# Moving low parts, layer norm sums and norm products from GpSimd to VectorE in a hybrid attention layer

## The chip, the cores and the metric

The kernel runs on one core of a Trainium2 chip. The metric is the device time of one execution, in microseconds (us). A run's time is what is compared; the profile below is of one execution, whose span (first to last instruction) is a little shorter than its time. TensorE's clock has two levels here, 1.2 and 2.4 GHz; the granted clock in the rows is the share of the higher one.

## What is computed

One decoder layer on x of 1024 tokens by 1024 channels in float32. From xn = RMSNorm(x) one projection w_in gives the inputs of three branches:

```
A: sparse attention: 8 query heads in 2 groups, RMS-normed q and k;
   compressed keys/values from blocks of 32 tokens (stride 16) through a small MLP,
   selected blocks (all 16 are taken at this length), and a window of 512; three gates
B: u = a * sigmoid(ag); causal depthwise convolution over 31 taps;
   LayerNorm over 512 channels; silu; projection
C: cross attention of 4 heads into 256 memory tokens, RMS-normed q and k
merged = gate_A * A + gate_B * B + gate_C * C;  h = x + merged @ w_out
out = h + (silu(hn @ w_gate) * (hn @ w_up)) @ w_down,  hn = RMSNorm(h)
```

## The kernel before

**Products in three parts.** A float32 operand is split into a high part (a cast to fp32r, on ScalarE, called ACT in the profile) and a low part (the operand minus the high part). `split` (L130) does both; the low part runs on VectorE unless an engine is given. `mm3` (L151) makes high x high, high x low and low x high, three matmuls for each product. A weight unit (`unit`, L246) is a DMA of 512 KB into a staging tile of two buffers (`st`, for the fill `fst` of one), a cast of 128x1024 and a low part of 128x1024. `col_unit` and `row_units` call it; `row_units` makes two units.

**Order of the work.** The kernel is written as one long list of steps. A planner (the Tile layer) lays the instructions of each engine out in one fixed order before the run, by a priority that follows the order of the text and by its own simulation of times. On the chip every engine works through its list in that order, and waits by semaphores. SyncE (SP) issues all DMAs, in its order too.

1. *Start.* The row norm_mix is loaded (L317 to L319), spread over the partitions by a matmul with ones and scaled by ACT into `gmix` (L324, L325). Four tiles of 256 tokens of x are loaded (L320, L327), normed (`norm_pair`, L200: square and sum on ACT, L205; scaling on VectorE, L207), transposed on TensorE (L216) and split. Along with it goes the projection of the first half of the memory queries.
2. *Convolution inputs* (L368): per channel tile two weight units, four projections, sigmoid, product on VectorE (L378).
3. *The taps.* 31 taps for each of four channel tiles (L361), 124 multiply-adds of some 128x1000 on VectorE (L364, L365), accumulate the convolution. They have a low priority (TAP) and are spread by hand over the following projections (L572 to L579): tap j is laid out after the matmul at which the share of columns passed reaches j / (124 + TAP_LEAD), TAP_LEAD = 24. The columns counted go from the end of the first channel tile to the last query projection.
4. *Compression* (L404 to L460): two weight units with low parts on GpSimd (POOL), additions of the positions (L417, L420, on GpSimd), the MLP.
5. *Memory* (L463 to L563): the memory tokens are normed and projected to keys and values by eight units, then two rounds of memory attention, beside which the remaining query projections run. The low parts of their units, the products of a norm with its gain (`gain_mul`, L292) and the scaling of the softmax (L521) are on GpSimd.
6. *Layer norm of the convolution* (L581 to L609): a sum over four channel tiles (`sum4`, L581, on GpSimd), the mean by a matmul with ones, subtraction (L593), squares, a second sum on GpSimd, the variance, products with the reciprocal root on GpSimd (L606), silu, and a DMA of the result.
7. *Keys and values* of the selected and window branches (L612 to L636), four units with low parts on GpSimd, eight gain products.
8. *Attention* (L639 to L768), with scalings on GpSimd (L653, L661).
9. *The fill* (L778 to L791): 24 units of the merge gate projection, each 48 matmuls of 512 columns (two halves of the tokens, 8 blocks of channels, 3 parts), with the lowest priority of all (FILL). The first N_EARLY = 12 go wherever TensorE has a gap; the others are spread over the attention by hand. Each unit's low part is on GpSimd. There are two buffers for fill units (`fsl`) and one PSUM bank (`pf`), copied out by ACT (L790).
10. Merge, output projection and the feed-forward part follow; nothing in them is changed.

```
def split(hi, lo, src, eng=None):
    nc.scalar.copy(hi, src)
    sub(eng or nc.vector, lo, src, hi.bitcast(F32))
...
        along = products[first_tap:]
        total, run, j = sum(n for _, n in along), 0, 0
        for m, n in along:
            while j < len(taps) and run * (len(taps) + TAP_LEAD) >= j * total:
```

Of the kernel before, what the change touches and what calls it, by code (L numbers as in the profile page):

```python
# [11 lines left out]
AF = mybir.ActivationFunctionType  # L12
OP = mybir.AluOpType
# [4 lines left out]
P = 128  # L18
S = 1024
D = 1024  # L20
# [8 lines left out]
C_Q, C_KC, C_VC, C_KV, C_G, C_A, C_AG, C_QM, C_GM = 0, 512, 640, 768, 1280, 1304, 1816, 2328, 2840  # L29
# [2 lines left out]
ORDER = mybir.DependencyInfo(mybir.DependencyClass.NoSync, mybir.DependencyReason.DATA)  # L32
N_EARLY = 12
WB, LAG, SPREAD = 6, 4, 97
TAP_LEAD = 24
N_MAIN, N_W, N_F = 16, 3, 2


# [1 line left out]
def hybrid_layer_kernel(  # L40
# [4 lines left out]
    nc = tc.nc  # L45
    x, mem, out = x[0], mem[0], out[0]
    w_in, w_mem_kv, w_out = w_in[0], w_mem_kv[0], w_out[0]
# [41 lines left out]
    def t2(shape, dt=F32, p=P):  # L89
        return t2p.tile([p] + shape, dt, tag="t2", name=nm("t2"))  # L90
# [135 lines left out]
    def rows2(src, r0):  # L226
        xs = slab([2, D], F32)
        for tt in range(2):
            nc.sync.dma_start(xs[:, tt, :], src[r0 + tt * P:r0 + (tt + 1) * P, :])
        return xs  # L230
# [25 lines left out]
    def col_unit(w, c0, n=P, alloc=wslab, eng=None, load=False):  # L256
        return unit(w[:, c0:c0 + n].rearrange("(k p) c -> p k c", p=P), [w.shape[0] // P, n], alloc, eng,
                    load)

    def row_units(w, c0, alloc=wslab, eng=None):  # L260
        return [unit(w[u * 512:(u + 1) * 512, c0:c0 + 256].rearrange("(k p) c -> p k c", p=P), [4, 256], alloc, eng)
                for u in range(2)]
# [7 lines left out]
    def tok_proj(ws, tp, act=xn, alloc=bank):  # L270
        o = alloc([2, 256])
        for tt in range(2):
            t = 2 * tp + tt
            half, a = t // 4, (t % 4) * P
            for k in range(KT):
                w = ws[k // 4]
                mm3(o[:, tt, :], act(0, k, half, a, a + P), act(1, k, half, a, a + P), w[:, 0, k % 4, :],
                    w[:, 1, k % 4, :], k == 0, k == KT - 1)
        return o
# [11 lines left out]

    def gain_mul(t, g):  # L292
        a, h, d = t.shape[1:]
        nc.gpsimd.tensor_tensor(t, t, g[:, None, None, :].to_broadcast([P, a, h, d]), op=OP.mult)


    def head_norms(raw, gain):
# [15 lines left out]
    def raw_proj(ws, tp, dest):  # L313
        ps = tok_proj(ws, tp).rearrange("p t (h d) -> p t h d", h=dest.shape[2])
        nc.scalar.copy(dest[:, 2 * tp:2 * tp + 2], ps)

    g1 = [t2([512], p=1) for _ in range(2)]  # L317
    for half in range(2):
        nc.sync.dma_start(g1[half], norm_mix[:, half * 512:(half + 1) * 512])  # L319
    xin = [rows2(x, 0)]  # L320
    gmix = t4([D])
    for half in range(2):
        b = bank([512])
        nc.tensor.matmul(b, ones[0:1, :], g1[half], start=True, stop=True)  # L324
        nc.scalar.activation(gmix[:, half * 512:(half + 1) * 512], b, AF.Copy, scale=512.0)  # L325
    ws = row_units(w_in, C_QM)
    xin += [rows2(x, tp * 256) for tp in range(1, 4)]  # L327
    nc.sync.dma_start(gm, mem_qk_norm.to_broadcast([P, 2, P]))
# [1 line left out]
    QMQ = {}  # L330
# [71 lines left out]


    def compress_in(kind, c0):  # L404
        w = col_unit(w_in, c0, eng=nc.gpsimd)
        raw = t4([2, 512])
        for half in range(2):
            ps = chan_proj(w, half)
            for g in range(2):
                for par in range(2):  # L410
                    o = raw[par * 64:(par + 1) * 64, g, half * 256:(half + 1) * 256]
                    i = ps[g * 64:(g + 1) * 64, par::2]
                    nc.scalar.copy(o, i)
        rv = raw.rearrange("p g (i m) -> p m g i", m=8)
        AB = slab([2, 8, 2, 64], F32)
        A, B = AB[:, 0], AB[:, 1]
        nc.gpsimd.tensor_tensor(A, rv, pos[:, kind, 0:8, None, None].to_broadcast([P, 8, 2, 64]), op=OP.add)  # L417
        nc.gpsimd.memset(B[:, :, :, 63:64], 0.0)
        for g in range(2):
            nc.gpsimd.tensor_tensor(B[:, :, g, 0:63], rv[:, :, g, 1:64],  # L420
                                    pos[:, kind, 8:16, None].to_broadcast([P, 8, 63]), op=OP.add)
        return A, B

# [48 lines left out]
    KM = slab([2, 4, 256])  # L472
    VM = slab([2, 2, 512])
    for hp in range(2):
        ps = tok_proj(row_units(w_mem_kv, hp * 256, eng=nc.gpsimd), 0, mn).rearrange("p t (h d) -> p t h d", h=2)
        kn = t2([2, 2, P])
        heads_norm(ps, kn)
        gain_mul(kn, gm[:, 1, :])
        b = bank([2, 256])
        for h in range(2):  # L480
            for tt in range(2):
                nc.tensor.transpose(b[:, h, tt * P:(tt + 1) * P], kn[:, tt, h, :], ident)
        split(KM[:, 0, 2 * hp:2 * hp + 2, :], KM[:, 1, 2 * hp:2 * hp + 2, :], b)
    for hp in range(2):
        ps = tok_proj(row_units(w_mem_kv, 512 + hp * 256, eng=nc.gpsimd), 0, mn)
        split(VM[:, 0, :, hp * 256:(hp + 1) * 256], VM[:, 1, :, hp * 256:(hp + 1) * 256], ps)

    msc = float(P) ** -0.5
# [57 lines left out]
    def mem_attention(hp, ws, dest):  # L546

        QM, pm = {0: mem_qT(hp, 0)}, {}
        for tp in range(5):
            if tp < 3:  # L550
                QM[tp + 1] = mem_qT(hp, tp + 1)
            if tp < 4:
                pm[tp] = mem_softmax(hp, tp, QM[tp])
                raw_proj(ws, tp, dest)
            if tp > 0:
                mem_out(hp, tp - 1, pm[tp - 1])

    QMQ[1] = slab([NT, 2, P], F32)
    mem_attention(0, row_units(w_in, C_QM + 256, eng=nc.gpsimd), QMQ[1])
    head_norms(QMQ[1], gm[:, 0, :])  # L560
    Q = [slab([NT, 4, 64], F32) for _ in range(2)]
    mem_attention(1, row_units(w_in, C_Q, eng=nc.gpsimd), Q[0])
    head_norms(Q[0], None)  # L563


    ws = row_units(w_in, C_Q + 256, eng=nc.gpsimd)
    for tp in range(4):
        raw_proj(ws, tp, Q[1])
    head_norms(Q[1], None)
# [11 lines left out]
    def sum4(part):  # L581
        for a, b_ in ((0, 1), (2, 3), (0, 2)):
            i0 = U[a][:, part] if (a, b_) != (0, 2) else U[0][:, 0]
            i1 = U[b_][:, part] if (a, b_) != (0, 2) else U[2][:, 0]
            nc.gpsimd.tensor_tensor(U[a][:, 0], i0, i1, op=OP.add)

    sum4(1)
    for half in range(2):
# [8 lines left out]
    for half in range(2):  # L597
        c = slice(half * 512, (half + 1) * 512)
        pv = bank([512])
        mm(pv, ones, U[0][:, 0, c], True, True)  # L600
        sd = t2([512])
        nc.scalar.activation(sd, pv, AF.Sqrt, scale=1.0, bias=LN_EPS)
        rs = t2([512])
        nc.vector.reciprocal(rs, sd)
        for ct in range(4):
            nc.gpsimd.tensor_tensor(U[ct][:, 1, c], U[ct][:, 1, c], rs, op=OP.mult)  # L606
    for ct in range(4):
        nc.scalar.activation(U[ct][:, 0], U[ct][:, 1], AF.Silu, scale=cw[:, ct, 32:33], bias=cw[:, ct, 33:34])
        nc.sync.dma_start(ud[ct], U[ct][:, 0])  # L609
# [2 lines left out]
    KS, KW = slab([2, S]), slab([2, S])  # L612
    VS, VW = slab([NT, 2, P]), slab([NT, 2, P])
    for s, K, V in ((0, KS, VS), (1, KW, VW)):
        ws = row_units(w_in, C_KV + s * 256, eng=nc.gpsimd)

        def keys(tp, cat):
            b = bank([2, 2, P], F32R)
            for j in range(4):
                nc.tensor.transpose(b[:, j // 2, j % 2, :], cat[:, j].rearrange("p a d -> p (a d)"), identr)  # L620
            nc.vector.tensor_copy(K[:, :, tp * 256:(tp + 1) * 256].rearrange("p g (t q) -> p t g q", t=2),
                                  b.bitcast(F32))

        last = None
        for tp in range(4):
            v = tok_proj(ws, tp).rearrange("p t (a g d) -> p t a g d", a=2, g=2)
            kn = t2([2, 2, 64])
            heads_norm(v[:, :, 0], kn)
            gain_mul(kn, gn[:, 2 + s, :])
            cat = t2([4, 2, 64], F32R)  # L630
            split(cat[:, :, 0, :], cat[:, :, 1, :], kn.rearrange("p t g d -> p (t g) d"))
            split(V[:, 2 * tp:2 * tp + 2, :, 0:64], V[:, 2 * tp:2 * tp + 2, :, 64:128], v[:, :, 1])
            if last is not None:
                keys(tp - 1, last)
            last = cat
        keys(3, last)  # L636
# [141 lines left out]
    with low(FILL):  # L778
        for n_ in range(3 * KT):
            b_, d_ = n_ // KT, n_ % KT  # L780
            w = col_unit(w_in, C_GM + b_ * D + d_ * P, alloc=fslab, eng=nc.gpsimd)
            for h_ in range(2):
                ps = fbank([512])
                for k in range(KT):
                    first = mm3(ps, w[:, 0, k, :], w[:, 1, k, :], xn(0, k, h_), xn(1, k, h_), k == 0, k == KT - 1)
                    j = ((n_ - N_EARLY) * 2 + h_) * KT + k
                    if j >= 0:
                        tc.add_manual_dep(first.ins, spread[j].name, ORDER, reason="spread over the attention")
                z = fzp.tile([P, 512], F32, tag="fz", name=nm("fz"))
                nc.scalar.copy(z, ps)  # L790
                nc.sync.dma_start(zd[b_, d_, :, h_ * 512:(h_ + 1) * 512], z)  # L791
# [383 lines left out]
```

## Time and profile before

| what | value |
|---|---|
| median of 3 runs | 1753.63 us (1752.31 to 1754.61) |
| the profiled execution, its time | 1751.1 us |
| its span | 1749.4 us |
| mean granted clock of TensorE | 0.994 |
| busy: PE / PEld / DVE / ACT / POOL | 1706.7 / 1482.7 / 1072.2 / 734.3 / 632.0 us |

The profile names the engines PE (TensorE's matmuls), PEld (its weight loads, which overlap them), DVE (VectorE), ACT (ScalarE), POOL (GpSimd) and SP (SyncE, which issues the DMAs); SPq is SyncE's queue of DMA issues. A row of the timeline gives start, duration, engine, line, operation, written tile <- read tiles, shape, and the count where several were merged; in brackets stands how long the engine had stood idle and what ended that. L131 and L128 are the lines of the high and the low part in `split` and `sub`, so they name the kind of work and not its place; the tiles tell the place (`wsl` and `fsl`: weight units, of the fill too; `slab`: activations; `t`: small tiles; `ps` and `pf`: PSUM).

### The profile page before, as it was taken

Reading aid. Unit: us, or ns where it says so; the run is one execution under the profiler, and the core shown is the slowest. Engines: PE = TensorE matmul, PEld = TensorE weight load, DVE = VectorE, ACT = ScalarE, POOL = GpSimd, SP = SyncE. Lnnn points to the kernel's source line nnn. Section 1 sums busy time; section 2 is a strip of 40 time slices with the busy share of each in tenths; the row PEclk is TensorE's granted clock in tenths of the full one; section 3 lists DMA queues with packets and bytes.
Section 4 is the critical chain, followed back from the end, with each engine's and each line's share of the span. In section 5 each row is a group of like instructions: output and inputs, shape, how many; then the busy total and the mean of one; then the engine's idle time right before and its main releaser. Section 6 shows DMA issues by size and latency. Waiting matters only on the chain. (4 is left out here: it accounts for less than half of the span.)

```text
span 1749.4 us, 25269 instructions
## 1 busy us (share of the span) xinstructions
PE 1706.7 (98%) x9483; PEld 1482.7 (85%) x9483; DVE 1072.2 (61%) x1813; ACT 734.3 (42%) x1380; POOL 632.0 (36%) x539
## 2 busy tenths in 40 slices
PE   6999799999999999999999999999999999999999
PEld 5887798998888889989888899788888888888887
DVE  5499988745355566766754623864545554457655
ACT  6211353344356566666653423642322223234332
POOL 1102574435344343434203500166556667410000
PEclk9999999999999999999999999999999999999999
DMA  6213332122112111111285322233333445794673
GB/s 202 56 28 96 127 108 74 43 61 76 45 58 71 55 49 40 49 34 53 79 305 199 129 73 98 78 108 109 96 113 104 151 147 167 248 395 155 228 228 128
DMA packets 178388, 204.08 MB, mean 117 GB/s; under 512 B 10774, under 2 KB 125750, under 8 KB 177242
## 3 DMA queue, kind: packets, MB, share of 16 engines
q1 hardware_dynamic: 178266, 202.47, 35.1%
q8 instruction: 74, 1.21, 0.3%
q14 instruction: 48, 0.39, 0.1%
HBM read 152.10 MB, written 50.33 MB: 116 GB/s over the span
## 5 line engine op out<-in xcount | busy, mean ns | idle before, releaser
L144 PE MATMUL ps<-slab,wsl 128*128 128x512 f32 (+1 forms) x1664 | 371.7, 382 | 3.0 <-DVE t L128 2.4
L144 PEld LDWEIGHTS ps<-slab,wsl 128*128 128x128 f32 x1664 | 303.3, 189 | 64.0 <-issue 2.6
L144 PE MATMUL pf<-slab,fsl 128*128 128x512 f32 x1236 | 323.9, 400 | 4.8 <-ACT fz L790 4.7
L144 PEld LDWEIGHTS pf<-slab,fsl 128*128 128x128 f32 x1236 | 224.0, 189 | 47.1 <-ACT fz L790 7.0
L144 PE MATMUL ps<-wsl,slab 128*128 128x256 f32 x1680 | 217.9, 285 | 0.0
L144 PEld LDWEIGHTS ps<-wsl,slab 128*128 128x128 f32 x1680 | 209.3, 193 | 2.2 <-issue 0.7
L365 DVE SCALAR_TENSOR_TENSOR slab<-slab,cw 128x1019 f32<-128x1019 f32 (+18 forms) x120 | 184.8, 1550 | 1.9
L1005 DVE TENSOR_TENSOR t<-ps,t 128x512 f32<-128x512 f32 x127 | 86.9, 688 | 112.1 <-PE ps L144 107.1
L144 PE MATMUL ps<-slab,fsl 128*128 128x512 f32 x636 | 147.7, 389 | 0.0
L128 DVE TENSOR_TENSOR t<-ps,t 128x512 fp32r<-128x512 f32 (+3 forms) x196 | 120.2, 631 | 34.6 <-ACT t L131 33.4
L144 PEld LDWEIGHTS ps<-slab,fsl 128*128 128x128 f32 x636 | 119.4, 188 | 24.8
L144 PE MATMUL ps<-t,slab 128*128 128x256 f32 x624 | 117.1, 293 | 2.9 <-DVE t L128 2.6
L1109 PE MATMUL ps<-wsl 128*128 128x512 f32 x495 | 118.5, 389 | 0.0
L131 ACT CAST t<-ps 128x512 fp32r<-128x512 f32 (+2 forms) x192 | 98.3, 542 | 46.2 <-PE ps L739 31.3
L1109 PEld LDWEIGHTS ps<-wsl 128*128 128x128 f32 x495 | 92.9, 188 | 19.3
L131 ACT CAST wsl<-st 128x1024 fp32r<-128x1024 f32 x65 | 68.4, 1053 | 84.5 <-PE ps L144 44.4
L144 PEld LDWEIGHTS ps<-t,slab 128*128 128x128 f32 x624 | 94.5, 191 | 10.1 <-DVE t L128 4.0
L128 POOL TENSOR_TENSOR wsl<-st,wsl 128x1024 fp32r<-128x1024 f32 x20 | 55.7, 2800 | 121.3 <-ACT wsl L131 121.2
L144 PE MATMUL ps<-slab,qt 128*128 128x384 f32 (+3 forms) x384 | 95.2, 340 | 0.0
L128 DVE TENSOR_TENSOR wsl<-st,wsl 128x1024 fp32r<-128x1024 f32 x45 | 62.0, 1379 | 42.4 <-ACT wsl L131 39.4
L653 POOL TENSOR_SCALAR wsl<-wsl,sm 128x640 f32<-128x640 f32 (+7 forms) x76 | 52.9, 709 | 94.9 <-DVE sm L651 37.6
L131 ACT CAST wsl<-t 128x1024 fp32r<-128x1024 f32 x42 | 44.3, 1056 | 97.4 <-POOL t L128 38.7
(233 smaller groups left out, 2809.9 us busy)
## 6 DMA issues: line engine op xcount, KB each, us to landing
t<-in_w_down_dram SPq DMA_DIRECT2D x70, 256.0 KB, 4.0
fst<-in_w_in_dram SPq DMA_DIRECT2D x24, 512.0 KB, 3.7
zd<-fz SPq DMA_DIRECT2D x48, 256.0 KB, 2.0
t<-zd SPq DMA_DIRECT2D x24, 512.0 KB, 4.0
st<-in_w_in_dram SPq DMA_DIRECT2D x22, 512.0 KB, 4.0
st<-in_w_gate_dram SPq DMA_DIRECT2D x22, 512.0 KB, 4.3
st<-in_w_up_dram SPq DMA_DIRECT2D x22, 512.0 KB, 4.1
ad<-t SPq DMA_DIRECT2D x44, 256.0 KB, 2.7
```

Source lines behind the costliest of these rows:

```text
L128: eng.tensor_tensor(o, a, b, op=OP.subtract)
L131: nc.scalar.copy(hi, src)
L144: m = nc.tensor.matmul(o, a, b, start=start, stop=stop)
L365: return nc.vector.scalar_tensor_tensor(acc[:, s:], u[:, :S - s], cw[:, ct, 30 - s:31 - s], acc[:, s:], op0=OP.mult, op1=OP.add)
L653: nc.gpsimd.tensor_scalar(tiles[h], tiles[h], c[:, h:h + 1], 1.0, op0=OP.mult, op1=OP.mult)
L1005: nc.vector.tensor_tensor(o, a_, b_, op=OP.add)
L1109: nc.tensor.matmul(B[t], a_, b_, start=start and k == 0 and j == 0, stop=k == FH - 1 and j == 2, skip_group_check=True)
```

## The change

Six kinds of instructions go from GpSimd to VectorE: the low parts of all weight units from compression to the keys and values (20 units), the additions of the positions, the products of norms with gains, the sums and products of the layer norm, and the low parts of the first 12 fill units (the other 12 stay on GpSimd). The spreading out of `gmix` goes from ACT to VectorE. TAP_LEAD becomes 12. The DMAs of the first tile of x are issued ahead of those of norm_mix.

```diff
-TAP_LEAD = 24
+TAP_LEAD = 12
...
     def gain_mul(t, g):
-        nc.gpsimd.tensor_tensor(t, t, g[:, None, None, :].to_broadcast([P, a, h, d]), op=OP.mult)
+        nc.vector.tensor_tensor(t, t, g[:, None, None, :].to_broadcast([P, a, h, d]), op=OP.mult)
...
+    xin = [rows2(x, 0)]
     g1 = [t2([512], p=1) for _ in range(2)]
     for half in range(2):
         nc.sync.dma_start(g1[half], norm_mix[:, half * 512:(half + 1) * 512])
-    xin = [rows2(x, 0)]
...
-        nc.scalar.activation(gmix[:, half * 512:(half + 1) * 512], b, AF.Copy, scale=512.0)
+        nc.vector.tensor_scalar(gmix[:, half * 512:(half + 1) * 512], b, 512.0, None, op0=OP.mult)
...
     def compress_in(kind, c0):
-        w = col_unit(w_in, c0, eng=nc.gpsimd)
+        w = col_unit(w_in, c0)
...
-        nc.gpsimd.tensor_tensor(A, rv, pos[:, kind, 0:8, None, None].to_broadcast([P, 8, 2, 64]), op=OP.add)
+        nc.vector.tensor_tensor(A, rv, pos[:, kind, 0:8, None, None].to_broadcast([P, 8, 2, 64]), op=OP.add)
...
-            nc.gpsimd.tensor_tensor(B[:, :, g, 0:63], rv[:, :, g, 1:64],
+            nc.vector.tensor_tensor(B[:, :, g, 0:63], rv[:, :, g, 1:64],
...
-        ps = tok_proj(row_units(w_mem_kv, hp * 256, eng=nc.gpsimd), 0, mn).rearrange("p t (h d) -> p t h d", h=2)
+        ps = tok_proj(row_units(w_mem_kv, hp * 256), 0, mn).rearrange("p t (h d) -> p t h d", h=2)
...
-    mem_attention(0, row_units(w_in, C_QM + 256, eng=nc.gpsimd), QMQ[1])
+    mem_attention(0, row_units(w_in, C_QM + 256), QMQ[1])
...
     def sum4(part):
-            nc.gpsimd.tensor_tensor(U[a][:, 0], i0, i1, op=OP.add)
+            nc.vector.tensor_tensor(U[a][:, 0], i0, i1, op=OP.add)
...
-            nc.gpsimd.tensor_tensor(U[ct][:, 1, c], U[ct][:, 1, c], rs, op=OP.mult)
+            nc.vector.tensor_tensor(U[ct][:, 1, c], U[ct][:, 1, c], rs, op=OP.mult)
...
-            w = col_unit(w_in, C_GM + b_ * D + d_ * P, alloc=fslab, eng=nc.gpsimd)
+            w = col_unit(w_in, C_GM + b_ * D + d_ * P, alloc=fslab,
+                         eng=nc.vector if n_ < N_EARLY else nc.gpsimd)
```

The values of memory (L485), the second round of memory attention (L562), the last query projection (L566) and the keys and values (L615) lose their `eng=nc.gpsimd` in the same way.

## Rows read from the trace of the kernel before

**Rows 1.** The page's first part: busy us, share of the span, instructions.

```profile
PE 1706.7 (98%) x9483; PEld 1482.7 (85%) x9483; DVE 1072.2 (61%) x1813; ACT 734.3 (42%) x1380; POOL 632.0 (36%) x539
```

**Rows 2.** Busy times by stretch: length, PE, PEld, DVE, ACT, POOL, clock, DMA share, GB/s.

```profile
0.00:20.00 20.00, 7.80 (x21) 4.44 (x22) 10.16 (x17) 11.79 (x22) 3.14 (x13) 1.00 0.90 316
...
180.00:300.00 120.00, 105.31 (x753) 98.64 (x752) 110.36 (x104) 48.48 (x101) 69.78 (x36) 0.96 0.32 101
...
340.00:480.00 140.00, 136.45 (x972) 126.36 (x971) 64.72 (x124) 58.11 (x123) 56.45 (x47) 0.99 0.17 57
480.00:880.00 400.00, 397.56 (x2469) 354.70 (x2468) 258.52 (x862) 250.67 (x615) 160.17 (x213) 1.00 0.18 57
```

**Rows 3.** TensorE's waits from 176 to 300 us: total us, times, longest.

```profile
PE ps L216 <- DVE slab L207: 9.0, 1, 9.0
PE ps L482 <- POOL t L294: 1.7, 1, 1.7
PE ps L144 <- DVE t L128: 1.6, 2, 1.2
PE ps L216 <- DVE kcmp L449: 1.5, 1, 1.5
PE ps L531 <- POOL t L521: 0.9, 1, 0.9
```

**Rows 4.** Timeline of VectorE ahead of the longest wait.

```profile
175.63 25.19 DVE L365 SCALAR_TENSOR_TENSOR slab<-slab,cw 128x1023 f32<-128x1023 f32 x12
```

**Rows 5.** TensorE's timeline at that wait, and the stretch's busy times.

```profile
192.15 3.69 PE L144 MATMUL pf<-slab,fsl 128*128 128x512 f32 x15
204.82 0.69 PE L216 MATMUL ps<-ident,slab 128*128 128x128 f32 x2 [8.98 <-DVE slab L207]
...
175.63:200.74 25.11, 20.21 (x156) 18.90 (x155) 24.93 (x13) 9.23 (x18) 17.65 (x6) 1.00 0.50 168
```

**Rows 6.** VectorE's busy time on L365 alone, in two stretches.

```profile
100.00:120.00 20.00, 16.25 (x13) 1.00 0.14 31
160.00:345.00 185.00, 119.91 (x72) 0.97 0.29 92
```

**Rows 7.** Low parts on GpSimd by shape: busy us, mean ns, idle before.

```profile
L128 POOL TENSOR_TENSOR wsl<-st,wsl 128x1024 fp32r<-128x1024 f32 x20 | 55.7, 2800 | 121.3 <-ACT wsl L131 121.2
```

**Rows 8.** VectorE: L309 on the timeline, and low parts away from GpSimd's work.

```profile
371.90 2.48 DVE L309 TENSOR_TENSOR slab<-slab,smw 128x512 f32<-128x512 f32 x4
...
L128 DVE TENSOR_TENSOR wsl<-slab,wsl 128x1024 fp32r<-128x1024 f32 x13 | 15.9, 1222 | 6.8 <-ACT wsl L131 6.8
```

**Rows 9.** Fill matmuls (tile pf) from 180 to 300 us, by engine.

```profile
180.00:300.00 120.00, 27.32 (x109) 20.12 (x110) 0.00 (x0) 2.38 (x4) 0.96 0.32 101
```

**Rows 10.** A stretch of 2 us after the longest wait, columns as in rows 2.

```profile
204.00:206.00 2.00, 1.18 (x6) 1.18 (x7) 1.96 (x4) 1.99 (x6) 0.52 (x1) 0.50 0.01 4
```

**Rows 11.** The start: timeline, and a DMA of the first 20 us.

```profile
0.80 0.64 SPq L319 DMA_DIRECT2D t<-in_norm_mix_dram  x2
1.49 0.83 SPq L229 DMA_DIRECT2D slab<-in_x_dram  x2
...
2.27 3.75 PE L324 MATMUL ps<-t,ones 1*128 1x512 f32 x4 [2.27 <-DMA t<-in_norm_mix_dram]
...
6.05 0.60 ACT L325 ACTIVATE t<-ps 128x512 f32<-128x512 f32 x1 [1.11 <-PE ps L324]
...
8.15 1.28 DVE L207 SCALAR_TENSOR_TENSOR slab<-slab,sm,t 128x1024 f32<-128x1024 f32 x1
...
12.22 1.29 DVE L207 SCALAR_TENSOR_TENSOR slab<-slab,sm,t 128x1024 f32<-128x1024 f32 x1
...
gm<-in_mem_qk_norm_dram SPq DMA_DIRECT2D x1, 128.0 KB, 10.1
```

**Rows 12.** The last tap, and the mean's matmuls, on the timeline.

```profile
340.88 1.25 DVE L365 SCALAR_TENSOR_TENSOR slab<-slab,cw 128x994 f32<-128x994 f32 x1
...
383.96 1.88 PE L144 MATMUL ps<-slab,ones 128*128 128x512 f32 x4
```

More of the change, by code (lines that the diff above doesn't have):

```diff
@@ L484, in hybrid_layer_kernel @@
     for hp in range(2):
-        ps = tok_proj(row_units(w_mem_kv, 512 + hp * 256, eng=nc.gpsimd), 0, mn)
+        ps = tok_proj(row_units(w_mem_kv, 512 + hp * 256), 0, mn)
         split(VM[:, 0, :, hp * 256:(hp + 1) * 256], VM[:, 1, :, hp * 256:(hp + 1) * 256], ps)
@@ L558, in hybrid_layer_kernel @@
     QMQ[1] = slab([NT, 2, P], F32)
-    mem_attention(0, row_units(w_in, C_QM + 256, eng=nc.gpsimd), QMQ[1])
+    mem_attention(0, row_units(w_in, C_QM + 256), QMQ[1])
     head_norms(QMQ[1], gm[:, 0, :])
     Q = [slab([NT, 4, 64], F32) for _ in range(2)]
-    mem_attention(1, row_units(w_in, C_Q, eng=nc.gpsimd), Q[0])
+    mem_attention(1, row_units(w_in, C_Q), Q[0])
     head_norms(Q[0], None)
-    ws = row_units(w_in, C_Q + 256, eng=nc.gpsimd)
+    ws = row_units(w_in, C_Q + 256)
     for tp in range(4):
@@ L614, in hybrid_layer_kernel @@
     for s, K, V in ((0, KS, VS), (1, KW, VW)):
-        ws = row_units(w_in, C_KV + s * 256, eng=nc.gpsimd)
+        ws = row_units(w_in, C_KV + s * 256)
         def keys(tp, cat):
```

## The prediction

> **What bounds the kernel now.** I read the busy times of the page first. TensorE is busy for 1706.7 of 1749.4 us [rows 1]. The matmuls stay the same in number, so a change of VectorE or GpSimd work can give back only time in which TensorE stands still or runs at the lower of its two clocks. That leaves 42.7 us of standstill, so the next question is where it lies. The busy times by stretch answer it [rows 2]: 12.2 us in the first 20, 14.7 us from 180 to 300, 3.6 us from 340 to 480, and only 2.4 us in the 400 us of attention. The change works up to attention, so it plays for the first three.
>
> Who ends the waits between 176 and 300 us? Five kinds do [rows 3], and the largest is one wait of 9.0 us for L207, the scaling of the memory tokens on VectorE. VectorE was not idle. It worked through 12 convolution taps in 25.19 us without a break [rows 4], 2.10 us for each, and L207 stood behind them in the same queue. TensorE ran out of fill at 195.84 and resumed at 204.82 [rows 5]. A tap does not cost 2.10 us by itself: between 100 and 120 us, with GpSimd idle, 13 took 16.25 us, 1.25 us each [rows 6]. During the 12 slow ones GpSimd was busy for 17.65 us with exactly the work that the change takes away [rows 5]. So I read the stall as VectorE slowed by GpSimd's two-input work on the same memory, while its queue was laid out for faster taps.
>
> **The change, part by part.** Prices on VectorE: 1.22 us for a low part of 128x1024 [rows 8], and 0.62 us for 128x512 from SBUF (four of L309 take 2.48 [rows 8]). The strided additions of compression (L417, L420) have no VectorE row. They lie between the 1.22 and 0.62 of the plain shape and the 2.80 us that GpSimd takes for as many elements [rows 7]; I take the plain shape, the row of the same engine.
>
> *VectorE's balance from 160 to 345 us.* Of the 20 weight low parts (2.80 us each on GpSimd [rows 7]) and the first fill low parts, 17 fall here: 17 x 1.22 = 20.7 us. Two L417, four L420, six gain products and one sum (the second moves out with the last taps) add 1.22 x 3 + 0.62 x 10 = 9.9 us. New work: 30.6 us. Freed: the 72 taps here take 119.91 us [rows 6], and 72 x 1.25 would be 90.0, so 29.9 us come back if every tap runs at its own speed; a tap can't lose more than that, and gives nothing back if something else slows it. Between the two ends I take the whole, as GpSimd is left with little two-input work. So moving the work is even. Then the pace: taps are released by the share of product columns passed, 124 of 124 + lead. With lead 24 they end at 84% of the columns, with 12 at 91%. Twelve or so (15 us) leave this stretch. They go to 345-372 us; VectorE is busy for 64.72 of 140 us from 340 to 480 [rows 2]. Their user, the mean over channels, is on TensorE only at 383.96, while the last tap began at 340.88 [rows 12]: this cover of 43 us shrinks to about 10. If it were gone, each late microsecond would count there.
>
> *The 9.0 us wait.* Its place is at half the columns (246,784 of 492,544 counted from the code). At half, 74 taps are released now and 68 after: 6 x 1.25 = 7.5 us less ahead of L207. The 12 slow taps lose 25.19 - 15.0 = 10.2 us. New ahead of it are one L417, two L420, one sum and two low parts, 6.1 us. Net 11.6 us earlier, more than the wait, so between 0 (the order is laid out anew and L207 stays late) and -9.0; I take -8.0.
>
> In the Trainium skill the page "SBUF — State Buffer", section "SBUF: two separate sides", says that VectorE and GpSimd share a port pair under an exclusive lock, so that one waits for the other's whole instruction. By that rule VectorE would get back GpSimd's full 17.65 us rather than 10.2, and the term would be the full -9.0. The trace agrees only in part: 12 x 1.25 + 17.65 = 32.7 us of work went through in 25.19 us.
>
> *The other waits.* kcmp (1.5) stood behind contended taps: -1.0. L482 (1.7) waited for a gain product on GpSimd, which becomes 0.62 us with perhaps one tap of 1.25 ahead: 0 to -1.7, I take -1.0. L531 and L144 (0.9 and 1.6) stand behind GpSimd low parts or slowed taps: 0 to -2.5, I take -1.4.
>
> *Clock.* After the longest wait TensorE ran at half clock, 0.50 from 204 to 206 us [rows 10]. From 180 to 300 us the granted clock is 0.96 of 120 us [rows 2], 4.8 us of clock lost. Part of that passed while TensorE stood, so I take half, -2.4 (0 to -4.8).
>
> *Start.* The tile of x is issued 0.7 us earlier and the two rows of norm_mix behind it [rows 11]. Now ACT stands until 6.05 us for the gain copies before it squares x. Afterwards it need not wait. But the gain's DMA lands behind 1 MB: at the 316 GB/s of the first 20 us [rows 2] that is 3.3 us, so near 5.3 by my estimate. Then come two products (3.75 us [rows 11]) and a VectorE copy: first L207 near 9.7 instead of 8.15, the second near 11.0 instead of 12.2. TensorE waits for the second: -1.2. Bounds: -2, and +5 if the row lands as late as gm did, 10.1 us after issue. I take -1.0.
>
> *New waits.* A low part or gain product at the head of its chain now meets a tap that can't be broken off: half a tap on the mean, 0.63 us. GpSimd could wait for ACT's cast with nobody urgent behind it; VectorE will have taps, L207 and the other low parts queued behind such a wait, and TensorE behind those. I count six chains short of cover (the two products at L482, the first loads of the four pairs from w_mem_kv): +3.8 (0 to +8). POOL's queue keeps the softmax scalings and loses what stood before them. SP issues the same transfers, as soon as staging buffers are free; with 1.22 for 2.80 us that is not later. Layer norm: the sums and products shrink by about 9 us, all beside projections: nothing.
>
> **Sum.** -8.0 - 1.0 - 1.0 - 1.4 - 2.4 - 1.0 + 3.8 = -11.0 against the profiled execution, 1751.1 us, so 1740.1. The median of the runs stands 2.5 us above that execution: **1742.6 us**.
>
> **The rivals.** *Everything goes* (10%): the five waits (14.7), the clock (4.8) and 2 us of the start, with no new wait: -21.5, 1732.1 us. For it speaks that VectorE's load falls by 15 us in its tightest stretch; against it that each gap filled so far showed another chain behind.
>
> *Nothing to measure* (18%): the planner releases taps otherwise than my count and L207 moves by 10.2 - 6.1 = 4.1 us only; L482 and L531 give 1.9, clock and start nothing, new waits cost 3.8: -2.2, 1751.4 us. For it: the work moved equals the time freed, so the queue can be as full as before.
>
> *Slower* (18%): the fill starves. Fill matmuls close 27.32 us of gaps from 180 to 300 us, 109 of them [rows 9], 12.0 us for a unit of 48. Their low parts were on a GpSimd with time to spare; now they have the lowest priority on VectorE, below the taps. If one and a half units come too late for this stretch, TensorE stands 18 us more (the matmuls move into attention, where there is no gap for them): 1742.6 + 18 = 1760.6 us. It decides where VectorE has no free 1.22 us between a fill unit's cast and its turn. For it: VectorE is busy for 110.4 of 120 us [rows 2]. Against it: the freed 30 us lie in the same stretch, and units are two buffers ahead.
>
> The change does what it says by its code; only the order that the planner makes of it is open, and the two rivals above are that.
>
> **How the numbers follow.** The forecast has 54%; its own range is 1736 to 1747. A measurement tells some 0.2% (3.5 us) from no change. Faster by more: the forecast but for its edge, and the first rival, 0.63. Within: the second rival and that edge, 0.19. Slower: 0.18. The range takes in the larger gain and the middle rival with its bounds and leaves out the starved fill: 1732 to 1756.
>
> **What would show it.** Taps near 1.25 us all through 160-345 us; L207 before 196 us and no wait of TensorE above 2 us from 180 to 300; GpSimd nearly empty before 460 us; the last tap near 370 us and the mean's matmuls still not waited for. Wrong, if taps run at 1.25 us and TensorE still waits: then the order or the fill decides, and fewer than 80 fill matmuls from 180 to 300 us beside longer gaps would be the third rival.

## The result and the profile after

The changed kernel takes 1736.78 us (median of 4 runs, 1736.27 to 1737.04) against 1752.97 us before (4 runs): a ratio of 0.9907 (95% interval [0.9895, 0.9919]), 16.2 us faster. The forecast was 1742.6 us, its range 1732 to 1756. The changed kernel's line numbers are those of before up to L780 and one more behind that. Its profiled execution took 1737.04 us with a span of 1735.3 us.

The page's first part, columns as in [rows 1]:

```profile
PE 1704.0 (98%) x9483; PEld 1480.1 (85%) x9483; DVE 1087.8 (63%) x1885; ACT 732.3 (42%) x1378; POOL 482.8 (28%) x469
```

The busy times by stretch, columns as in [rows 2]:

```profile
0.00:20.00 20.00, 7.65 (x20) 4.29 (x20) 10.00 (x17) 10.10 (x18) 3.13 (x13) 1.00 0.91 321
...
180.00:300.00 120.00, 119.44 (x843) 110.86 (x842) 102.57 (x120) 54.06 (x108) 11.24 (x16) 1.00 0.38 119
...
340.00:480.00 140.00, 139.62 (x990) 129.57 (x989) 90.47 (x167) 60.18 (x130) 12.49 (x20) 1.00 0.19 61
480.00:880.00 400.00, 392.40 (x2430) 349.20 (x2429) 265.25 (x866) 253.46 (x612) 152.20 (x208) 1.00 0.20 65
```

The gain can be booked from these rows and [rows 1, 2]: the span is TensorE's busy time plus its standstill.

| TensorE, us | before | after | difference |
|---|---|---|---|
| standstill 0 to 20 | 12.20 | 12.35 | +0.15 |
| standstill 180 to 300 | 14.69 | 0.56 | -14.13 |
| standstill 340 to 480 | 3.55 | 0.38 | -3.17 |
| standstill 480 to 880 | 2.44 | 7.60 | +5.16 |
| standstill elsewhere | 9.82 | 10.41 | +0.6 |
| busy, at the clock granted | 1706.7 | 1704.0 | -2.7 |
| span | 1749.4 | 1735.3 | -14.1 |

The stretch that the prediction pointed at is nearly full, and its clock went from 0.96 to 1.00. Attention gave 5.2 us back, a loss that the prediction did not have. The 3.2 us from 340 to 480 us lie mostly in the fill's waits for its copies out of PSUM; TensorE's waits from 300 to 480 us, before and then after:

```profile
PE pf L144 <- ACT fz L790: 4.2, 4, 2.4
```

```profile
PE pf L144 <- ACT fz L791: 1.1, 2, 0.7
```

From 176 to 300 us the view of TensorE's waits, which had five kinds [rows 3], has one row left:

```profile
PE ps L448 <- DVE t L128: 0.3, 1, 0.3
```

What filled the gaps is seen in the fill's own busy times (tile pf; columns length, PE, PEld, DVE, ACT, clock, DMA share, GB/s), in the changed kernel:

```profile
180.00:300.00 120.00, 44.96 (x179) 32.56 (x180) 0.00 (x0) 4.09 (x7) 1.00 0.38 119
480.00:880.00 400.00, 187.12 (x695) 124.16 (x693) 0.00 (x0) 16.87 (x29) 1.00 0.20 65
```

and in the kernel before, for the second stretch (the first is [rows 9], 109 matmuls):

```profile
480.00:880.00 400.00, 210.89 (x792) 141.59 (x792) 0.00 (x0) 19.27 (x33) 1.00 0.18 57
```

So 70 more fill matmuls run in the old gaps, and 97 fewer are left for attention (23.8 us less of fill in the same 400 us). This is how standstill saved at 200 us shortens the end at 1750: work that may go anywhere goes earlier. Whether less fill is also why attention stands still 5.2 us more is not shown. Two of the waits there are new, in the view of TensorE's waits from 480 us on:

```profile
PE ps L144 <- DVE sm L707: 1.9, 3, 1.3
PE ps L665 <- POOL t L661: 1.8, 2, 0.9
```

But two of the runs below have nearly as much fill in this stretch as the kernel before (792 matmuls, 2.4 us of standstill) and still stand longer: the products alone with 789 matmuls 5.7 us, the run with 40 additions with 767 matmuls 6.4 us.

The taps on VectorE alone (L365), columns as in [rows 6], and the two scalings of the memory tokens. The first of them ended the 9.0 us wait in the kernel before, where it began at 203.49 us:

```profile
160.00:345.00 185.00, 82.34 (x66) 1.00 0.31 99
```

```profile
193.77 1.27 DVE L207 SCALAR_TENSOR_TENSOR slab<-slab,sm,t 128x1024 f32<-128x1024 f32 x1
...
199.81 1.27 DVE L207 SCALAR_TENSOR_TENSOR slab<-slab,sm,t 128x1024 f32<-128x1024 f32 x1
```

A tap costs 1.25 us there, where 72 had cost 1.67 us each [rows 6]. The prices of the moved work on VectorE (group, busy us, mean ns, idle before):

```profile
L128 DVE TENSOR_TENSOR wsl<-st,wsl 128x1024 fp32r<-128x1024 f32 x27 | 33.3, 1232 | 19.7 <-ACT wsl L131 19.5
...
L420 DVE TENSOR_TENSOR slab<-t,pos 128x504 f32<-128x504 f32 x4 | 4.4, 1103 | 0.0
L417 DVE TENSOR_TENSOR slab<-t,pos 128x1024 f32<-128x1024 f32 x2 | 4.2, 2094 | 0.0
```

### The profile page after: what moved, and what is told of

Same layout as the page of the kernel before. It is cut to its first block, busy times and chain, and to the rows that moved or that the text cites. A ratio compares the mean times of both kernels' runs of the same rounds, so it can differ in the third digit from the quotient of the medians.

```text
span 1735.3 us, 25240 instructions
## 1 busy us (share of the span) xinstructions
PE 1704.0 (98%) x9483; PEld 1480.1 (85%) x9483; DVE 1087.8 (63%) x1885; ACT 732.3 (42%) x1378; POOL 482.8 (28%) x469
## 5 line engine op out<-in xcount | busy, mean ns | idle before, releaser
L144 PE MATMUL pf<-slab,fsl 128*128 128x512 f32 x1236 | 321.5, 399 | 1.2 <-ACT fz L791 1.1
L365 DVE SCALAR_TENSOR_TENSOR slab<-slab,cw 128x1023 f32<-128x1023 f32 (+15 forms) x120 | 151.4, 1266 | 1.8
L128 DVE TENSOR_TENSOR wsl<-st,wsl 128x1024 fp32r<-128x1024 f32 x65 | 84.7, 1303 | 53.5 <-ACT wsl L131 50.4
L521 POOL TENSOR_SCALAR t<-t,sm 128x256 f32<-128x256 f32 x32 | 22.5, 722 | 288.1 <-DVE sm L517 288.1
L1110 PE MATMUL ps<-fsl 128*128 128x512 f32 x330 | 79.8, 389 | 0.0
```

Of the source, the lines that this page charges most:

```text
L128: eng.tensor_tensor(o, a, b, op=OP.subtract)
L144: m = nc.tensor.matmul(o, a, b, start=start, stop=stop)
L365: return nc.vector.scalar_tensor_tensor(acc[:, s:], u[:, :S - s], cw[:, ct, 30 - s:31 - s], acc[:, s:], op0=OP.mult, op1=OP.add)
L521: nc.gpsimd.tensor_scalar(pm[:, tt, h, :], pm[:, tt, h, :], rec[:, j:j + 1], 1.0, op0=OP.mult, op1=OP.mult)
L1110: nc.tensor.matmul(B[t], a_, b_, start=start and k == 0 and j == 0, stop=k == FH - 1 and j == 2, skip_group_check=True)
```

## The experiments

Twelve runs were made. The kernel before was timed beside each group, and its median lay between 1752.4 and 1753.7 us, so differences between runs of different groups are known to about 1 us. In brackets behind a time stand its ratio to the kernel before and the 95% interval of that. The kernels with unused GpSimd work have other line numbers: taps L360, memory scaling L202, position additions L412 and L415.

**Does GpSimd's work slow VectorE by itself?** The changed kernel gets GpSimd work that nobody reads; to have room for it, the attention mask's strip is written behind it.

```diff
-    nc.gpsimd.memset(strip, 0.0)
...
+    for _ in range(45):
+        nc.gpsimd.tensor_tensor(strip[:, 0:512], U[3][:, 0, 0:512], U[3][:, 0, 512:1024], op=OP.add)
+    nc.gpsimd.memset(strip, 0.0)
```

The second kernel has 110 `tensor_scalar` of the same size in place of the 45 additions.

> The changed kernel with 45 additions of two 128x512 float32 tiles on GpSimd that nobody uses, placed after the compression inputs (from about 141 to 230 us). The order on every other engine is the same. Theory (GpSimd's two-input work slows VectorE's taps, and that made the 9.0 us wait): taps beside them take 1.8 to 2.1 us instead of 1.27, L207 comes 6 to 12 us later, TensorE waits for it again, and the time is 1743 to 1751 us. Rival (the gain is the shorter way of the moved work and the new order; sharing is harmless): 1736.8 us within 2 us.

> The same place and about the same GpSimd busy time, but 110 scalings of one 128x512 tile instead of additions of two. Theory as I put it (two-input work slows VectorE): taps 1.25 to 1.45 us, time within 2 us of 1736.8. Rival (any GpSimd instruction that reads the same memory holds VectorE up, as the Trainium skill's page SBUF - State Buffer, section SBUF: two separate sides, has it): taps 1.8 us and more, time as with the additions, 1743 to 1751 us.

Measured: 1773.07 us (1.0112 [1.0097, 1.0127]) and 1769.14 us (1.0087 [1.0072, 1.0102]). As totals these two tell nothing apart, and the fault is in how they were made: GpSimd works in order, and needed work stood behind the unused. In the first run no wait for that shows; TensorE's three longest waits from 176 to 300 us are the same, to 0.1 us, as in the repeat with 40 additions below. In the second run two of TensorE's waits are

```profile
PE ps L533 <- POOL t L523: 16.6, 2, 16.1
PE ps L144 <- POOL slab L413: 7.9, 1, 7.9
```

a softmax scaling and the clearing of one column for compression, both behind unused scalings, which ran until 286 us. So both were made again, with fewer copies and that clearing on VectorE:

```diff
-        nc.gpsimd.memset(B[:, :, :, 63:64], 0.0)
+        nc.vector.memset(B[:, :, :, 63:64], 0.0)
...
+    for _ in range(40):
+        nc.gpsimd.tensor_tensor(strip[:, 0:512], U[3][:, 0, 0:512], U[3][:, 0, 512:1024], op=OP.add)
```

and 60 `tensor_scalar` in the other.

> The changed kernel with 40 unused GpSimd additions of 128x512 from the last channel slab, before the compression products. Unlike the earlier run with 45 of them, the clearing of B's last column now stands on VectorE, so that nothing which TensorE needs queues behind them on GpSimd, and they should end by 236 us, before the first softmax scaling at 252 us. They use no result and wait for nothing but the slab; the strip's mask is made behind them, long before its use. Contention theory (two-operand work of GpSimd slows VectorE by itself): the additions take about 2.1 us each, from 149 to 235 us, taps beside them 2.0 to 2.2 us in place of 1.2; VectorE loses 30 to 35 us of its own work there, TensorE's waits on VectorE come back, and 1746 to 1757 us result. Queue theory (the gain came from taking low parts and products out of GpSimd's queue, where they stood behind one another): unused additions hold up nobody, so 1735.5 to 1738.5 us.

> The same with 60 unused GpSimd scalings of 128x512 (one operand) in place of the 40 additions, at some 1.4 us each from 139 to about 225 us: GpSimd is as busy for as long. If only work with two operands slows VectorE, taps stay within 1.2 to 1.3 us and the time within 1735.5 to 1739.5 us. If any GpSimd work on this memory does, taps take 1.6 us or more and the time comes to within 3 us of the run with additions.

Measured: 1770.85 us (1.0094 [1.0076, 1.0112]) with the additions and 1748.42 us (0.9966 [0.9955, 0.9977]) with the scalings, 34.1 and 11.6 us above the changed kernel. VectorE's and GpSimd's groups with the additions, from 150 to 237 us and from 140 to 240 us:

```profile
L415 DVE TENSOR_TENSOR slab<-t,pos 128x504 f32<-128x504 f32 x4 | 8.2, 2039 | 0.0
L412 DVE TENSOR_TENSOR slab<-t,pos 128x1024 f32<-128x1024 f32 x2 | 5.8, 2921 | 0.0
L128 DVE TENSOR_TENSOR wsl<-st,wsl 128x1024 fp32r<-128x1024 f32 x3 | 5.8, 1928 | 0.0
```

```profile
L455 POOL TENSOR_TENSOR strip<-slab 128x512 bf16<-128x512 f32 x40 | 85.0, 2125 | 149.9 <-DVE slab L373 146.8
```

The taps there (L360 alone, columns as in [rows 6]), with additions and with scalings:

```profile
150.00:237.00 87.00, 56.38 (x27) 0.82 0.26 89
```

```profile
140.00:223.00 83.00, 50.33 (x34) 0.94 0.34 115
```

A tap takes 2.09 us beside additions and 1.48 us beside scalings, against 1.23 us in the same windows of the changed kernel. The queue theory is out: work that nobody waits for brings TensorE's waits back, the old one (here L202) with its old size among them:

```profile
PE ps L144 <- issue: 13.9, 2, 10.8
PE ps L211 <- DVE slab L202: 9.1, 1, 9.1
PE ps L443 <- DVE t L128: 4.1, 1, 4.1
```

The longest, 10.8 us, the view puts down to nobody ("issue"). It ended 0.1 us behind a position addition on VectorE, whose result the compression's matmuls read, so it points at VectorE too:

```profile
198.79 2.92 DVE L412 TENSOR_TENSOR slab<-t,pos 128x1024 f32<-128x1024 f32 x1
...
201.81 3.76 PE L144 MATMUL ps<-slab,wsl 128*128 128x128 f32 x16 [10.76 <-issue]
```

The additions cost more than either theory gave. Against the same lines of the changed kernel VectorE lost 36 us beside them: 27 taps 23.1, six position additions 5.4, four low parts 3.0, two scalings 1.9 and three others 2.9. TensorE's standstill over the span grew by 27.5 us and its busy time by 6.3 us; the granted clock from 180 to 300 us was 0.87. Beside the scalings VectorE lost 13.2 us in the same way of counting (36 taps 7.8, the rest 5.3), and TensorE 9.3 and 1.9 us. So VectorE's queue took up only some 2 us of either loss between 140 and 240 us. The expectation for the scalings missed as well: one operand slows VectorE too, by some three tenths of what two do to a tap.

**Which part of the change pays?** The kernel before with the 20 weight units' low parts moved alone (`eng=nc.gpsimd` taken from `compress_in`, both `w_mem_kv` loops, the memory attentions, the last query projection and the keys and values), and with the products alone:

```diff
-        nc.gpsimd.tensor_tensor(t, t, g[:, None, None, :].to_broadcast([P, a, h, d]), op=OP.mult)
+        nc.vector.tensor_tensor(t, t, g[:, None, None, :].to_broadcast([P, a, h, d]), op=OP.mult)
```

with L417, L420, L585 and L606 changed in the same way.

> The kernel before with only the 20 weight units' low parts on VectorE; position additions, sums, norm products and the gains' products stay on GpSimd, the fill's low parts too, the lead stays 24 and the start as it was. Contention theory: the 12 slow taps ran beside position additions and low parts alike; the low parts' share of GpSimd's two-operand work goes (56 us over the stage), the additions stay. The wait for L207 shrinks by half at most (3 to 5 us), the other waits by 1 to 3: 1744 to 1749 us. Rival (VectorE's load alone decides, 24 us are added to its queue and no taps put off): the waits on VectorE grow, 1754 to 1762 us.

> The kernel before with only the position additions, sums, norm products and gain products on VectorE; every low part stays on GpSimd, the lead stays 24 and the start as it was. Contention theory: about a third of GpSimd's two-operand work before 345 us goes; the waits that came through gain products go, the wait for L207 shrinks in part: 1745 to 1750 us, and with the run that moves the weights alone the two gains add up to at most that of the whole change (16 us) less 1 us. Rival (the parts need each other, as VectorE's queue gets its room only when the last contention goes): both stay at 1750 us or above.

Measured: 1746.91 us (0.9960 [0.9945, 0.9976]) for the weights, 1753.20 us (1.0003 [0.9993, 1.0012]) for the products. The first gains 6.5 us, as expected; the second gains nothing, which is a miss for the theory that every contended instruction counts alike. The wait for L207 shows why neither is enough, first with the weights, then with the products (waits from 176 to 300 us):

```profile
PE ps L216 <- DVE slab L207: 5.2, 1, 5.2
```

```profile
PE ps L216 <- DVE slab L207: 6.1, 2, 3.2
PE ps L144 <- DVE slab L128: 3.3, 1, 3.3
PE ps L448 <- DVE t L128: 1.8, 1, 1.8
```

With the products on VectorE and the low parts still on GpSimd, the taps stay slow (109.01 us for 71 from 160 to 345 us) and VectorE has the additions on top, at 2.12 and 1.12 us. This trace is of an execution 4.5 us above its kernel's median, so its waits may be longer than usual.

**The lead of the taps.** The changed kernel with the old lead, the old kernel with the new one:

```diff
-TAP_LEAD = 12
+TAP_LEAD = 24
```

```diff
-TAP_LEAD = 24
+TAP_LEAD = 12
```

> The changed kernel with the taps' lead back at 24. Load theory (from 150 to about 300 us VectorE's own queue is what TensorE waits for, and each microsecond put into it or taken out of it there ends up in the time; both runs with unused GpSimd work agree with it: the additions took 35 us of VectorE's time and cost 34.1, the scalings took 11.6 and cost 11.6): the 6 taps more before the middle, 12 more before 345 us, put 7.5 to 15 us back into the queue, so 1744 to 1752 us, with the L207 wait back and under 150 fill matmuls from 180 to 300. Contention theory alone (the lead only lays out the same work otherwise; with taps at 1.25 us there is room for them): 1736 to 1739 us.

> The kernel before with the lead of 12 and nothing else. Load theory: the slow taps cost about 2 us each there, so 6 to 12 of them put off take 9 to 20 us out of VectorE's queue before 345 us, and 1736 to 1745 us result: most of the change's gain by one number. Contention theory alone: the taps still meet GpSimd's two-operand work, and the time stays at 1749 to 1754 us.

Measured: 1749.70 us (0.9981 [0.9972, 0.9991]) with the lead undone, 1745.96 us (0.9965 [0.9952, 0.9978]) with the lead alone. Without its lead the change keeps some 3 of its 16 us; alone, the lead gives 6.4 us, between the two theories' figures. The stretch from 180 to 300 us with the lead undone, columns as in [rows 2]:

```profile
180.00:300.00 120.00, 113.97 (x802) 105.76 (x801) 109.44 (x124) 51.90 (x105) 12.15 (x16) 0.97 0.37 115
```

Taps run at 1.25 us there too (88.44 us for 71 from 160 to 345 us), so contention is gone; there are only five more of them, 6.1 us, and VectorE is busy for 109.4 instead of 102.6 us. TensorE's standstill grew by 5.5 us from 180 to 480 us and its busy time by 5.1 us in all, in part by the lower clock. The L207 wait did not come back by name: from 176 to 300 us TensorE waits 3.9 us for the softmax scaling and 2.2 us for a compression tile, and 145 fill matmuls fit in, not 179. Both waits go back to VectorE: GpSimd's scaling (L521) itself waited for VectorE's L517, and the tile on ACT stood behind a cast that waited for VectorE's L444, which began at 197.48 us, 193.58 in the changed kernel. With the lead alone, L207 keeps 3.9 us of its 9.0.

One more thing stands in these numbers: at the old lead all moves together (1749.70 us) are slower than the weights' low parts alone (1746.91). The new start accounts for one to two of these 2.8 us, by the runs on it below, and at that lead the other moves gain nothing. The weights with the new lead and nothing else were not run, so how much of the change is needed is open.

**The fill's low parts** back on GpSimd, the rest as changed:

```diff
-                         eng=nc.vector if n_ < N_EARLY else nc.gpsimd)
+                         eng=nc.gpsimd)
```

> The changed kernel with the first 12 fill units' low parts back on GpSimd, the rest as it is. Some 7 of them fall before 345 us: VectorE gets rid of 7 x 1.2 us, and loses about 1.0 us on an instruction beside each low part on GpSimd. Load theory: even within 2 us, 1735 to 1739 us. If the fill units' place in VectorE's queue was what fed the 179 fill matmuls from 180 to 300 us (that a low part came in the queue's own order), the fill thins out there and 1740 to 1746 us result.

Measured: 1740.17 us (0.9931 [0.9916, 0.9946]), 3.4 us slower than with them on VectorE, just inside the second of the two ranges. The fill is thinner (161 matmuls from 180 to 300 us), and TensorE waits for softmax scalings on GpSimd, which low parts now stand ahead of or slow; which of the two weighs more is not settled. The waits from 176 to 300 us:

```profile
PE ps L531 <- POOL t L521: 2.8, 2, 1.5
PE ps L448 <- DVE t L128: 0.3, 1, 0.3
```

**The start.** The changed kernel with the start as it was before, and with norm_mix first but its copies on VectorE:

```diff
-    xin = [rows2(x, 0)]
     g1 = [t2([512], p=1) for _ in range(2)]
     for half in range(2):
         nc.sync.dma_start(g1[half], norm_mix[:, half * 512:(half + 1) * 512])
+    xin = [rows2(x, 0)]
...
-        nc.vector.tensor_scalar(gmix[:, half * 512:(half + 1) * 512], b, 512.0, None, op0=OP.mult)
+        nc.scalar.activation(gmix[:, half * 512:(half + 1) * 512], b, AF.Copy, scale=512.0)
```

The second kernel has only the first half of this edit.

> The changed kernel with norm_mix loaded first again and the gain copies on ACT again; the order differs only in the first 25 TensorE entries. Theory (the new start costs TensorE 1 to 1.5 us, because the gain rows land behind the 1 MB tile): first projection matmul near 20.3 us instead of 21.9, time 1735.3 to 1736.1 us. Rival (the later work hides or pays for it): 1736.8 us or more.

> The changed kernel with norm_mix loaded first, the gain copies still on VectorE. Theory (the late gain rows are the whole cost of the new start, the freed ACT a gain): norm_mix lands near 2.3 us, ACT squares the first tile near 5 us instead of 6.55 in the kernel before, first projection matmul 18.5 to 19.5 us, time 1733.8 to 1735.2 us. Rival (x lands later and the later loads set the start): first projection matmul after 20 us, time 1735.5 to 1737 us.

Measured: 1735.63 us (0.9898 [0.9881, 0.9914]) with the start undone, 1734.55 us (0.9893 [0.9878, 0.9908]; 1734.09 to 1735.04) with the order alone undone. The new start costs one to two microseconds where it was to give one. Both times fell into the range of the theory, but the first projection matmul of the second kernel came at 20.02 us, later than the 18.5 to 19.5 expected. The timeline of the changed kernel shows how:

```profile
5.74 3.75 PE L324 MATMUL ps<-t,ones 1*128 1x512 f32 x4 [5.74 <-DMA t<-in_norm_mix_dram]
7.82 0.69 DVE L325 TENSOR_SCALAR t<-ps 128x512 f32<-128x512 f32 x1 [5.23 <-PE ps L324]
9.19 1.23 DVE L128 TENSOR_TENSOR wsl<-st,wsl 128x1024 fp32r<-128x1024 f32 x1 [0.68 <-ACT wsl L131]
10.41 0.67 DVE L325 TENSOR_SCALAR t<-ps 128x512 f32<-128x512 f32 x1
...
11.00 1.22 DVE L128 TENSOR_TENSOR wsl<-st,wsl 128x1024 fp32r<-128x1024 f32 x1
...
12.13 1.28 DVE L207 SCALAR_TENSOR_TENSOR slab<-slab,sm,t 128x1024 f32<-128x1024 f32 x1
...
21.92 2.48 PE L144 MATMUL ps<-wsl,slab 128*128 128x256 f32 x10
```

The gain's rows land 3.5 us later than before (5.74 instead of 2.27 us). The products with ones end at 9.49 us, but the second copy stands on VectorE behind a low part until 10.41, and another low part is laid out between the copy and the first L207, which starts at 12.13 us instead of 8.15 [rows 11]. With norm_mix first, the copies are done at 6.82 us, just ahead of the first L207:

```profile
6.13 0.69 DVE L325 TENSOR_SCALAR t<-ps 128x512 f32<-128x512 f32 x1 [1.01 <-PE ps L324]
...
6.93 1.28 DVE L207 SCALAR_TENSOR_TENSOR slab<-slab,sm,t 128x1024 f32<-128x1024 f32 x1
...
20.02 3.94 PE L144 MATMUL ps<-wsl,slab 128*128 128x256 f32 x21
```

**Still fewer taps early?** The kernel just shown (norm_mix first, copies on VectorE) with a lead of 8:

```diff
-TAP_LEAD = 12
+TAP_LEAD = 8
```

> The run with the rows of norm_mix first and copied by VectorE (1734.6 us), with a lead of 8 besides. From 180 to 480 us TensorE stands still for 1.6 us in the changed kernel, so taking still more out of VectorE's queue can give 1.5 us at most: 1733 to 1735 us. If the cover of the mean over channels is gone (last tap now at 364.5 us, the mean's matmuls at 382.9 us; some 4 taps more move behind it), 1735 to 1740 us.

Measured: 1738.83 us (0.9921 [0.9906, 0.9936]), 4.3 us slower than with 12. The last tap starts at 371.0 instead of 364.5 us and the layer norm's last sum at 377.7 instead of 368.3. TensorE puts 24 fill matmuls ahead of the mean's and waits 3.8 us for the fill's copies from 300 to 480 us. The busy times, columns as in [rows 2]:

```profile
340.00:480.00 140.00, 136.93 (x954) 126.06 (x952) 90.24 (x159) 56.45 (x117) 11.22 (x18) 0.99 0.18 61
```

The cover of the mean over channels is nearly gone: the last sum ends at 378.9 us, and with a lead of 12 the mean's matmuls began at 380.95. That this is what the 4.3 us pay for is a reading; the view names no wait for the sum, only those for the fill's copies. Of the three leads tried, 12 is the best. The fastest version tried is therefore the changed kernel with norm_mix loaded first, at 1734.55 us.

## Why the prediction was right, and where not

The mechanism stood: VectorE, slowed beside GpSimd and carrying too much before 345 us, was late for TensorE, and the fill closed what gaps it could. The forecast was 5.8 us too high, about half by the terms (-11.0 forecast, -14.1 between the two profiled executions) and half by the 2.5 us put on top: the profiled execution after was the slowest of its four runs, 0.3 us above the median, so an offset of one kernel's profiled run did not carry over to the other's. That the terms came within 3.1 us is partly luck: from 180 to 300 us they were 6.5 us short (-7.6 forecast with the new waits, -14.1 measured), and the 5.2 us lost in attention, which they did not have, took most of that back.

*VectorE's balance* held: taps at 1.25 us gave back about 30 us, 72 x (1.665 - 1.248), where 29.9 was put. The position additions were taken at the plain shape's 1.22 and 0.62 us and cost 2.09 and 1.10, 3.7 us more in all, yet nothing waited. Eight taps lie behind 345 us, not twelve; the last one starts at 364.5 us, near the 370 put.

*The waits.* All five of [rows 3] went but for 0.3 us, 14.4 where 11.4 was forecast (-8.0, -1.0, -1.0 and -1.4). The step that failed here is *new waits*, +3.8 us for six chains that would meet a tap on VectorE: from 180 to 300 us there is 0.56 us of standstill in all. None of the six shows by name even with the lead undone, when VectorE is fuller. My reading, not shown by itself, is that the chains have room for half a tap once VectorE is not late.

*The lead* was priced only as a part of the wait for L207 (7.5 us of it). By the runs it decides most of the gain once the work has moved: 12.9 us go without it. At the old lead the moved work gains some 3 us, so it pays in full only when taps leave VectorE too, which the sentence "So moving the work is even" did not say as a condition. Put one at a time, weights (6.5), products (0) and lead (6.4) give 12.9 of the 16.2 us; since the parts act on one queue, such a sum need not hold.

*Clock*: -2.4 forecast; TensorE's busy time fell by 2.7 us over the whole span, and how much of that is the clock was not separated. *Start*: -1.0 forecast, and it costs +1 to +2. The gain row's landing (5.74 us, estimated 5.3) and the products (3.75 us) were right. The step that failed is the first L207, put at 9.7 us and measured at 12.13: two low parts share VectorE's queue there, one ahead of the second copy (0.9 us) and one behind it (some 1.1 us), which is the kind of cost that the paragraph on new waits named for elsewhere. *Not in the sum at all*: 3.2 us gained from 340 to 480 us, and 5.2 us lost in attention.

*The rivals.* The fill did not starve: 179 matmuls, not under 80, and the experiment with its low parts back on GpSimd says that VectorE was the better place for them. The case of nothing to measure comes close to what the change would be without its lead (1749.7 us; that rival's 1751.4).

*The weighing of the rule.* The prediction found that GpSimd's 17.65 us and the taps' 15.0 us went through in 25.19 us, and took that as speaking in part against the Trainium skill's page "SBUF — State Buffer", section "SBUF: two separate sides", by which one of the two engines waits for the other's whole instruction. That reading was flawed: GpSimd's 17.65 us hold its own waiting (two of its low parts there took 3.34 us each, against 2.39 in the row below). The kernel before shows the bare case elsewhere, on the timelines of GpSimd and VectorE:

```profile
398.73 2.39 POOL L128 TENSOR_TENSOR fsl<-fst,fsl 128x1024 fp32r<-128x1024 f32 x1 [0.41 <-ACT fsl L131]
...
407.56 10.07 POOL L606 TENSOR_TENSOR slab<-slab,t 128x512 f32<-128x512 f32 x8 [6.44 <-DVE t L604]
```

```profile
398.79 2.88 DVE L309 TENSOR_TENSOR slab<-slab,smw 128x512 f32<-128x512 f32 x1
```

A product that takes VectorE 0.62 us [rows 8] began 0.06 us behind a low part on GpSimd and took 2.88 us, until 0.55 us after the low part's end: it waited for all of it, as the page has it. In the run with 40 additions, taps and additions pass at some 2.1 us each, nearly in turn; eight products of the additions' size take GpSimd 1.26 us each without such company (L606 above), so strict turns would be 1.25 + 1.26 = 2.51 us, and by this estimate some 0.4 us still overlap. (The unused additions write bf16 and L606 float32, and no run has the additions by themselves.) For instructions of GpSimd with one operand the runs do not bear out a wait for the whole instruction: a tap loses 0.25 us beside scalings of 1.33 us on the mean. The number that the sum used, 10.2 us for the slow taps, came from the taps' own rows and stood.

## What to carry to other kernels

When two engines slow each other, price a move by what the receiving engine gets back from its own slowed instructions, and then look for what must leave its queue to make room; here that second number, one constant, was worth as much by itself (6.4 us) as the best single move (6.5 us), and without it all moves together kept 3 of the 16 us. A gap closed early pays at the end only as far as later stages do not give it back, so book the standstill stretch by stretch before and after. A busy time measured beside a rival engine holds waiting; take the price from a place where the engine is alone.

## What was not expected of the hardware

Scalings on GpSimd, with a single tensor operand, slow VectorE too, by 0.25 us for a tap of 1.23 us, where additions of two add 0.86 us. VectorE's position additions, which read their operand at a stride, cost 2.09 us for 128x1024 and 1.10 us for 128x504, against 1.23 us for a plain 128x1024 low part. And a standstill of TensorE came with more than itself: with the lead undone, 7.2 us more of standstill over the span went with 5.1 us more of busy time for the same 9483 matmuls, 4.4 us of it in the fill's (325.9 instead of 321.5 us for 1236). The lower granted clock from 180 to 300 us (0.97 against 1.00) is one part of that; what else adds to it is open, since elsewhere the changed kernel had stretches at a lower clock as well (0.88 from 650 to 660 us).
